# Second parts of split weights on GpSimd alone, tangents of the silu in PSUM, in a two-block transformer kernel

## The chip, the cores and the metric

The kernel runs on one core of a Trainium2 chip. The metric is the device time of one execution, in microseconds (us). Three runs of the kernel before took 2133.84, 2142.33 and 2143.69 us; their median is 2142.33 us.

## What is computed

One call runs two transformer blocks on 256 tokens of width 1024. The first block is a mixer made of a gated delta rule (GDN, 8 heads) and a state space layer (SSD, 16 heads), then a mixture of 32 experts. The second is a sparse attention with a gated linear attention, then 32 smaller experts. Everything is float32. The change lies in the first mixer, of which this much matters:

```python
proj = h @ w_in                                   # 256 x 1024 by 1024 x 6688
qkv = jax.nn.silu(causal_dwconv(gdn_qkv, gdn_conv_w))   # 3072 channels, 4 taps
q, k = l2norm(q) * (GDN_DK ** -0.5), l2norm(k)
o = gated_delta_rule_chunked(q, k, v, beta, g)    # 4 chunks of 64 tokens, a state passes on
o = rmsnorm(o, gdn_norm_g) * jax.nn.silu(gdn_z)
xbc = jax.nn.silu(causal_dwconv(ssd_xbc, ssd_conv_w) + ssd_conv_b)   # 1536 channels
y = ssd_chunked(xs, dt, a, bm, cm) + ssd_d * xs
return jnp.concatenate([o, rmsnorm(y * jax.nn.silu(ssd_z))], -1) @ w_out
```

The silu is computed as y(1 + tanh y), with y half of the convolution's result (the factor is put into the taps).

## The kernel before

**Split weights.** A float32 product is made of three matmuls in a faster type (`fp32r`): each operand is split into a first part (`wh`, `hT0`) and a rest (`wl`, `hT1`), and `mm3` adds first by first, first by rest and rest by first. `hT` is the transposed input, split once. The weights arrive in chunks of 1 MB, 128 x 2048 in SBUF (`w`). `splitter` cuts a chunk into `NSPL` = 4 parts of 512 columns: for each, ScalarE (ACT) writes `wh`, a rounded copy (L295), and then VectorE (DVE) or GpSimd (POOL) writes `wl` = `w` - `wh` (L292). `k.spd` names the parts that DVE does; it comes from the table `SPD`, one entry for each stage of the program. The first three entries hold up to the recurrence of the delta rule, and there parts 1 and 2 go to DVE and parts 0 and 3 to POOL. `wh` and `wl` have `NWH` = 2 buffers each, and a chunk is split one ahead of its use: the first piece of chunk i+2 waits until TensorE (PE) is through with chunk i.

**Stages up to the recurrence.** 23 chunks are split there. Six hold the 12 channel groups of the SSD (`xbc`), eight the keys and queries (16 groups of 128 channels), four the gate of the SSD, four the values (8 groups), and one is split ahead for the stage behind. For a chunk with two groups PE makes 48 matmuls into a PSUM tile `ps_pj` (3 buffers, `PJ`); then `conv_silu` runs once for each group.

**`conv_silu`** (L649). ACT scales the projection by the last tap (`cv_y`, L295), three DVE instructions add the other taps (L658: one input in PSUM, one in SBUF), ACT takes the tangent (`cv_t`, L295, two SBUF buffers), and DVE makes the product (L661: both inputs, `cv_t` and `cv_y`, in SBUF). PE then transposes the result (L730 for `xT`, L821 for `qk`, L1019 for `vT`), and the banks of these transposes, as of almost all small matmuls, come from a ring of five PSUM banks (`bank`, tag `g`). With `ps_pj` that is all eight banks.

**Beside it.** `ada_batch` accumulates 16 chunks of another weight on DVE (L478, 128 x 2048, both inputs in SBUF). `ssd` multiplies masks (`m`, L781 and L292) and on POOL scales `xs` and `xw`. `gdn_prep` inverts triangular blocks by doubling, a chain PE (32 x 32 matmuls, `Yc`, `Xc`, `Qc`) - DVE - PE. `weave` and `turns` interleave these generators with the projections in the text of the program; when it is built, a scheduling layer lists each engine's instructions in its own order, from the same dependences. Each engine then works through its list in order: an instruction that waits holds all behind it.

**After it.** The recurrence (`gdn_steps`), the output projection and the router follow, then the experts, whose weights stream from HBM; the second block has the same two halves.

Of the kernel before, what the change touches and what calls it, by code (L numbers as in the profile page):

```python
# [12 lines left out]
F32 = mybir.dt.float32  # L13
# [8 lines left out]
P = 128  # L22
T = 256
# [219 lines left out]
def turns(*gens):  # L243

    gens = list(gens)
    while gens:
        for g in list(gens):
            if next(g, gens) is gens:
                gens.remove(g)
        yield  # L250


def chain(*gens):
    for g in gens:
        yield from g


def weave(main, *sides):

    due = [0.0] * len(sides)  # L260
    for _ in main:
        for i, (g, rate) in enumerate(sides):
            due[i] += rate
            while due[i] >= 1:
                due[i] -= 1
                next(g, None)


def kernel_body(ctx, tc, ins, consts, out):
# [96 lines left out]
    def splitter(pool):  # L366
        def f(w):
            hi = pool.tile([P, W_CHUNK], F32R, tag="wh", bufs=NWH, name="wh")[:, :w.shape[1]]
            lo = pool.tile([P, W_CHUNK], F32R, tag="wl", bufs=NWH, name="wl")[:, :w.shape[1]]
            n = w.shape[1] // NSPL  # L370
            for i in range(NSPL):
                c = slice(i * n, (i + 1) * n)
                split_into(w[:, c], hi[:, c], lo[:, c], eng=None if i in k.spd else nc.gpsimd)
            return hi, lo
        return f

    ws.splitter = splitter(pA)
    k.spd = SPD[0]

# [173 lines left out]
    gcp = pc.tile([P, KD], F32, name="gcp")  # L553
    k.__dict__.update(locals())
    mixer1(k)
    pA.end(0)
    ps_cm.__exit__(None, None, None)
# [26 lines left out]
def mixer1(k):  # L584
    nc, tc, ws, pA = k.nc, k.tc, k.ws, k.pA
    mm, mm3, tt, act, bank, C, ident = k.mm, k.mm3, k.tt, k.act, k.bank, k.C, k.ident
# [59 lines left out]
        nc.gpsimd.tensor_copy(ac2[:, :, c:c + 16], acum)  # L646


    def conv_silu(pj, wc, ct, nct, dst, bias=None):  # L649

        y = pA.tile([P, T], F32, tag="cv_y", bufs=2, name="cv_y")
        w = lambda j: wc[:, j * nct + ct:j * nct + ct + 1]
        if bias is None:
            act(y, pj, AF.Copy, scale=w(3))
        else:
            act(y, pj, AF.Identity, scale=w(3), bias=bias)
        for s in (1, 2, 3):
            V.scalar_tensor_tensor(y[:, s:], pj[:, :T - s], w(3 - s), y[:, s:], op0=ALU.mult, op1=ALU.add)  # L658
        th = pA.tile([P, T], F32, tag="cv_t", bufs=2, name="cv_t")
        act(th, y, AF.Tanh)  # L660
        V.scalar_tensor_tensor(dst, th, 1.0, y, op0=ALU.add, op1=ALU.mult)  # L661

    def proj_ch(n, emit, emit2=None):

        for i in range(n):
            w = ws.get(split=True)
            pj = bank("pj", PJ)
            for ct in range(2):
                for kk in range(KD):
                    sl = slice(kk * 256 + ct * P, kk * 256 + ct * P + P)  # L670
                    mm3(pj[:, ct * T:(ct + 1) * T], (w[0][:, sl], w[1][:, sl]), (hT[0][:, kk], hT[1][:, kk]), start=(kk == 0), stop=(kk == KD - 1))
                if ct == 0:
                    yield
            if emit:
                for ct in range(2):
                    emit(2 * i + ct, pj[:, ct * T:(ct + 1) * T])
            else:
                emit2(i, pj)
            yield
# [44 lines left out]
    def emit(c, pj):  # L724
        if c < 8:
            xT = pA.tile([P, T], F32, tag="vT", bufs=2, name="xT")
            conv_silu(pj, cws, c, 12, xT, bias=hb[:, c:c + 1])
            pt = bank()
            for t in range(2):
                nc.tensor.transpose(pt[:, t * P:(t + 1) * P], xT[:, t * P:(t + 1) * P], ident)  # L730
                act(xs[t][:, c * P:(c + 1) * P], pt[:, t * P:(t + 1) * P], AF.Copy)
        else:
            conv_silu(pj, cws, c, 12, bc[:, c - 8], bias=hb[:, c:c + 1])
# [81 lines left out]
    def emit_kq(a):  # L815
        def f(h, pj):
            dst = qkv(h)[:, a].rearrange("p n s -> p (n s)")
            conv_silu(pj, cwg, h + (0 if a else 8), 24, dst)
            pt = bank()
            for t in range(2):  # L820
                nc.tensor.transpose(pt[:, t * P:(t + 1) * P], dst[:, t * P:(t + 1) * P], ident)  # L821
                jk = pA.tile([P, P], F32, tag="jk", bufs=1, name="jk")
                act(jk, pt[:, t * P:(t + 1) * P], AF.Square, accum_out=ssq[:, t, a * 8 + h:a * 8 + h + 1])
                if a == 0:
                    act(kd[t][:, h * P:(h + 1) * P], pt[:, t * P:(t + 1) * P], AF.Copy)
        return f
    k.spd = SPD[1]
    weave(turns(chain(proj_ch(4, emit_kq(0)), proj_ch(4, emit_kq(1))), ssd()), (ada1, RA[1]))
    run_all(ada1)
    ys = xs  # L830
    k.spd = SPD[2]

# [276 lines left out]

    k.spd = SPD[3]  # L1110
    fill = chain(proj_ch(4, None, emit_z), ssd_out)
# [6 lines left out]

    k.spd = SPD[4]

# [726 lines left out]
def mixer2(k, pool):  # L1847
# [9 lines left out]
    ws.splitter = k.splitter(pool)  # L1857
    k.spd = SPD[5]

# [690 lines left out]
NA4 = 17  # L2550
PJ = 3
NSPL = 4
SPD = ((1, 2),) * 3 + ((1, 2, 3), (1, 3), (), (1, 2), (1, 2))
RA = (0.34, 0.4, 0.25, 0.3)
FILL1 = 0.8
FILL2 = 0.6
# [55 lines left out]
```

## Time and profile before

| what | value |
|---|---|
| median of the runs | 2142.33 us |
| profiled execution, its own time | 2139.73 us |
| span of its profile | 2138.0 us |
| PE, DVE, ACT, POOL busy | 1906.9, 695.8, 438.1, 255.2 us |
| busiest split groups, whole program | POOL `wl` 180.8 us, DVE `wl` 112.4 us, ACT `wh` 139.7 us |
| HBM read | 703.69 MB, 330 GB/s over the span |

The profile is that of one execution. Busy time is what an engine's instructions took; in its share of the whole span DVE seems to have room, but most of DVE's work lies in the first 430 us and in the second mixer, while the experts between and behind them are made by PE and the weight stream. A stage is therefore read from its own stretch of the trace: who is busy there, and whom PE waits for.

### The profile page before, as it was taken

What the parts mean: (1) busy time and instruction counts of PE and PEld (TensorE: products, weight loads), DVE (VectorE), ACT (ScalarE), POOL (GpSimd) and SP (SyncE); (2) the same over time, 40 slices, a digit from 0 to 9 for tenths busy, and PEclk for the clock granted to TensorE, in tenths of its full rate; (3) what the DMA queues carried; (4) which work ended last, traced back from release to release, by engine and by line L of the source; (5) the groups of instructions that cost most, each with busy time, mean ns of one, the idle gap of its engine ahead of it and who ended that gap; (6) DMA issues with size and microseconds to landing.
All of it is one profiled execution on the core that took longest, in us unless ns stands there. A gap on an engine that the chain in (4) does not pass through costs nothing. (4 is left out here: it accounts for less than half of the span.)

```text
span 2138.0 us, 26656 instructions
## 1 busy us (share of the span) xinstructions
PE 1906.9 (89%) x10864; PEld 983.4 (46%) x10865; DVE 695.8 (33%) x1434; ACT 438.1 (20%) x1031; POOL 255.2 (12%) x202
## 2 busy tenths in 40 slices
PE   6889899699999999999999999979898788777777
PEld 3777788443343433434343433368787322212111
DVE  4988847511111211111111111375756200000001
ACT  3554524221010100001010100233543210101001
POOL 2523312200000000000000000144443000000000
PEclk8999979899999999999999999989999899999989
DMA  8654415689999999999999999936248699999997
GB/s 310 210 190 132 153 65 175 279 353 421 421 420 421 413 421 420 386 421 421 417 421 382 421 422 421 367 99 197 80 126 352 259 421 421 420 421 420 420 421 281
DMA packets 162552, 706.59 MB, mean 330 GB/s; under 512 B 20775, under 2 KB 67412, under 8 KB 87668
## 3 DMA queue, kind: packets, MB, share of 16 engines
q1 hardware_dynamic: 162420, 704.78, 83.0%
q8 instruction: 89, 1.46, 0.3%
q14 instruction: 43, 0.35, 0.0%
HBM read 703.69 MB, written 1.05 MB: 330 GB/s over the span
## 5 line engine op out<-in xcount | busy, mean ns | idle before, releaser
L282 PE MATMUL ps_gu<-w,xe 128*64 128x512 f32 (+1 forms) x3072 | 702.5, 629 | 67.8 <-DMA w<-in_w_up_dram 39.4
L282 PEld LDWEIGHTS ps_gu<-w,xe 128*64 128x64 f32 (+1 forms) x3072 | 227.6, 132 | 511.9 <-issue 373.3
L282 PE MATMUL ps_y<-w,aT 128*64 128x512 f32 (+1 forms) x1536 | 375.1, 602 | 14.8 <-DMA w<-in_w_down_dram 14.0
L292 POOL TENSOR_TENSOR wl<-w,wh 128x512 fp32r<-128x512 f32 x126 | 180.8, 1443 | 362.6 <-ACT wh L295 345.3
L282 PEld LDWEIGHTS ps_y<-w,aT 128*64 128x64 f32 (+1 forms) x1536 | 115.5, 128 | 234.1 <-issue 183.4
L1624 DVE TENSOR_SCALAR g<-ps_gu 128x512 f32<-128x512 f32 x32 | 22.0, 687 | 464.2 <-PE ps_gu L282 463.4
L295 ACT ACTIVATE wh<-w 128x512 fp32r<-128x512 f32 x244 | 139.7, 622 | 87.0 <-PE ps_pj L282 52.4
L282 PE MATMUL ps_pj<-hT,wh 128*128 128x256 f32 x704 | 143.3, 299 | 7.6 <-DVE cv_y L658 3.5
L292 DVE TENSOR_TENSOR wl<-w,wh 128x512 fp32r<-128x512 f32 x118 | 112.4, 972 | 46.0 <-ACT wh L295 42.4
L282 PEld LDWEIGHTS ps_pj<-hT,wh 128*128 128x128 f32 x704 | 116.6, 201 | 13.3 <-issue 5.5
L292 DVE TENSOR_TENSOR x<-x,ps_g 128x512 f32<-128x512 f32 x96 | 66.0, 687 | 168.1 <-PE ps_g L282 168.1
L282 PE MATMUL ps_pj<-hT,wl 128*128 128x256 f32 x352 | 105.3, 299 | 5.2 <-DVE wl L292 2.8
L295 ACT ACTIVATE g<-g 128x512 f32<-128x512 f32 x32 | 20.1, 629 | 417.9 <-DVE g L1624 417.2
L282 PE MATMUL ps_g<-ys,sgT 128*128 128x512 f32 x192 | 93.6, 616 | 1.6 <-DVE ys L292 0.8
L292 DVE TENSOR_TENSOR a<-g,ps_gu 128x512 f32<-128x512 f32 x8 | 5.5, 687 | 259.2 <-PE ps_gu L282 259.2
L282 PE MATMUL ps_g<-sel,xo 128*128 128x256 f32 x320 | 77.9, 392 | 2.0 <-ACT xe L295 1.7
L295 ACT ACTIVATE xe<-ps_g,mcol,a 128x256 f32<-128x256 f32 (+1 forms) x72 | 38.1, 539 | 190.8 <-PE ps_gu L282 150.0
L282 PEld LDWEIGHTS ps_pj<-hT,wl 128*128 128x128 f32 x352 | 71.0, 202 | 7.0 <-DVE wl L292 2.9
L282 PE MATMUL ps_pj<-uT,wh 128*128 128x256 f32 x384 | 74.0, 293 | 0.0
L292 DVE TENSOR_TENSOR ys<-ps_y,gb 128x512 f32<-128x512 f32 x32 | 22.1, 692 | 158.7 <-PE ps_y L282 158.7
L282 PEld LDWEIGHTS ps_g<-sel,xo 128*128 128x128 f32 x320 | 56.0, 189 | 31.8 <-ACT xe L295 13.3
L282 PEld LDWEIGHTS ps_pj<-uT,wh 128*128 128x128 f32 x384 | 61.5, 197 | 2.8 <-issue 1.2
(537 smaller groups left out, 1964.6 us busy)
## 6 DMA issues: line engine op xcount, KB each, us to landing
w<-in_moe_w_gu_dram SPq DMA_DIRECT2D x256, 1024.0 KB
w<-in_moe_w_down_dram SPq DMA_DIRECT2D x120, 1024.0 KB
w<-in_w_gate_dram SPq DMA_DIRECT2D x64, 1024.0 KB
w<-in_w_up_dram SPq DMA_DIRECT2D x64, 1024.0 KB
w<-in_w_down_dram SPq DMA_DIRECT2D x64, 1024.0 KB
w<-in_w_in_dram SPq DMA_DIRECT2D x45, 1024.0 KB
w<-in_ada_w_dram SPq DMA_DIRECT2D x24, 1024.0 KB
w<-in_w_out_dram SPq DMA_DIRECT2D x12, 1024.0 KB
```

Of the source, the lines that this page charges most:

```text
L282: return nc.tensor.matmul(o, l, r, start=start, stop=stop)
L292: (eng or nc.vector).tensor_tensor(o, a, b, op=op)
L295: nc.scalar.activation(o, i, f, **kw)
L1624: V.tensor_scalar(g, gu[j], 7.0, None, op0=ALU.min)
```

## The change

The tangent of `conv_silu` goes into a PSUM bank instead of an SBUF tile: a bank of the ring of five is taken for each pair of groups, the even group uses its first 256 columns, the odd one its second. And the first three entries of `SPD` become empty: up to the recurrence POOL writes `wl` of all four parts.

```diff
+    th2 = []
+
     def conv_silu(pj, wc, ct, nct, dst, bias=None):
...
-        th = pA.tile([P, T], F32, tag="cv_t", bufs=2, name="cv_t")
+        if ct % 2 == 0:
+            th2[:] = [bank()]
+        th = th2[0][:, ct % 2 * T:(ct % 2 + 1) * T]
         act(th, y, AF.Tanh)
         V.scalar_tensor_tensor(dst, th, 1.0, y, op0=ALU.add, op1=ALU.mult)
...
-SPD = ((1, 2),) * 3 + ((1, 2, 3), (1, 3), (), (1, 2), (1, 2))
+SPD = ((),) * 3 + ((1, 2, 3), (1, 3), (), (1, 2), (1, 2))
```

In the built program line numbers behind L645 move by two to four (L658 is L660, L661 is L665, L821 is L825). The order of each engine's list changes up to the recurrence and is the same behind it. Three places:

**POOL at the start**, from the first chunk on: `wl` are the weights' second parts, `hT` those of the input, which PE needs for its first chunk. Before:

```order
L292 TENSOR_TENSOR wl<-w,wh 128x512 x3
L292 TENSOR_TENSOR hT_235<-h_154,hT_234 128x256 x2
L292 TENSOR_TENSOR wl<-w,wh 128x512
L292 TENSOR_TENSOR hT_235<-h_155,hT_234 128x256 x2
L292 TENSOR_TENSOR wl<-w,wh 128x512 x3
```

Now:

```order
L292 TENSOR_TENSOR wl<-w,wh 128x512 x7
L292 TENSOR_TENSOR hT_235<-h_154,hT_234 128x256 x2
L292 TENSOR_TENSOR wl<-w,wh 128x512
L292 TENSOR_TENSOR hT_235<-h_155,hT_234 128x256 x2
L292 TENSOR_TENSOR wl<-w,wh 128x512 x8
```

Seven splits instead of three stand ahead of the first two pieces of `hT`.

**DVE at the first keys** (`qk` is the product of the silu, `bt` and `cbt` are copies for the SSD, `w<-w,cact` is the accumulation of `ada_batch`). Before:

```order
L658 SCALAR_TENSOR_TENSOR cv_y<-ps_pj,col_w,cv_y 128x254
L292 TENSOR_TENSOR wl<-w,wh 128x512
L661 SCALAR_TENSOR_TENSOR qk_868<-cv_t,cv_y 128x256
L658 SCALAR_TENSOR_TENSOR cv_y<-ps_pj,col_w,cv_y 128x253
L292 TENSOR_TENSOR wl<-w,wh 128x512
L751 COPY bt<-ps_g 128x128
L478 SCALAR_TENSOR_TENSOR w<-w,cact 128x2048
L751 COPY bt<-ps_g 128x128
L658 SCALAR_TENSOR_TENSOR cv_y<-ps_pj,col_w,cv_y 128x255
L292 TENSOR_TENSOR wl<-w,wh 128x512
L658 SCALAR_TENSOR_TENSOR cv_y<-ps_pj,col_w,cv_y 128x254
L292 TENSOR_TENSOR wl<-w,wh 128x512
```

Now:

```order
L665 SCALAR_TENSOR_TENSOR qk_862<-ps_g,cv_y 128x256
L755 COPY bt<-ps_g 128x128
L660 SCALAR_TENSOR_TENSOR cv_y<-ps_pj,col_w,cv_y 128x255
L660 SCALAR_TENSOR_TENSOR cv_y<-ps_pj,col_w,cv_y 128x254
L755 COPY bt<-ps_g 128x128
L660 SCALAR_TENSOR_TENSOR cv_y<-ps_pj,col_w,cv_y 128x253
L478 SCALAR_TENSOR_TENSOR w<-w,cact 128x2048
L765 COPY cbt<-ps_g 128x512
```

The splits are gone from DVE's list, and the product reads PSUM (`ps_g`).

**ACT at the last SSD groups** (`wh` are first parts of the next chunks). Before:

```order
L295 ACTIVATE wh<-w 128x512 x4
L295 ACTIVATE cv_t<-cv_y 128x256 x2
L295 ACTIVATE wh<-w 128x512 x2
L295 ACTIVATE cv_y<-ps_pj,hb,col_w 128x256
L295 ACTIVATE cv_y<-ps_pj,col_w 128x256
```

Now:

```order
L295 ACTIVATE wh<-w 128x512 x2
L295 ACTIVATE ps_g<-cv_y 128x256 x2
L295 ACTIVATE wh<-w 128x512 x3
L295 ACTIVATE cv_y<-ps_pj,hb,col_w 128x256
L295 ACTIVATE cv_y<-ps_pj,col_w 128x256
```

Two tangents stand side by side, and they now go into the PSUM ring.

## Rows read from the trace of the kernel before

**Rows 1.** The page's first line: span and instructions.
```profile
span 2138.0 us, 26656 instructions
```

**Rows 2.** Busy time by stretch: stretch, length; each engine's busy us (instructions); clock, DMA, GB/s.
```profile
36.00:60.00 24.00, 22.98 (x155) 19.49 (x154) 19.16 (x42) 11.09 (x24) 7.46 (x7) 0.93 0.77 256
60.00:100.00 40.00, 34.45 (x284) 33.05 (x283) 36.63 (x59) 24.23 (x62) 23.33 (x16) 1.00 0.63 212
100.00:140.00 40.00, 29.90 (x193) 26.04 (x192) 37.20 (x56) 20.65 (x63) 15.54 (x11) 0.87 0.64 211
140.00:195.00 55.00, 50.89 (x313) 40.76 (x312) 46.41 (x92) 34.83 (x105) 17.50 (x13) 1.00 0.35 115
195.00:270.00 75.00, 63.62 (x1397) 56.76 (x1399) 63.19 (x117) 33.81 (x83) 23.74 (x15) 0.93 0.49 156
...
430.00:1380.00 950.00, 934.23 (x3711) 369.60 (x3707) 160.48 (x294) 78.95 (x145) 5.68 (x7) 0.99 1.00 412
```
Engines in the row's order: PE, PE's weight loads, DVE, ACT, POOL.

**Rows 3.** Whom PE waited for from 36 to 270 us: us in total, times, longest.
```profile
PE ps_g L821 <- DVE qk L661: 6.4, 4, 4.6
PE ps_g L282 <- DVE Yc L292: 5.8, 2, 3.1
PE ps_pj L282 <- DVE cv_y L658: 3.5, 3, 2.3
...
PE ps_pj L282 <- DVE wl L292: 2.8, 1, 2.8
PE ps_g L1019 <- DVE vT L661: 2.5, 2, 1.4
PE ps_pj L282 <- POOL wl L292: 2.4, 1, 2.4
```

**Rows 4.** DVE's groups from 36 to 270 us: busy us, mean ns | idle before.
```profile
L658 DVE SCALAR_TENSOR_TENSOR cv_y<-ps_pj,col_w,cv_y 128x253 f32<-128x253 f32 (+2 forms) x108 | 48.6, 473 | 3.3 <-ACT cv_y L295 1.4 <-PE ps_g L1019 1.3
L292 DVE TENSOR_TENSOR wl<-w,wh 128x512 fp32r<-128x512 f32 x47 | 44.7, 958 | 2.1 <-ACT wh L295 1.5 <-issue 0.6
L478 DVE SCALAR_TENSOR_TENSOR w<-w,cact 128x2048 f32<-128x2048 f32 x11 | 25.8, 2343 | 2.0 <-DMA w<-in_ada_w_dram 2.0
...
L661 DVE SCALAR_TENSOR_TENSOR qk<-cv_t,cv_y 128x256 f32<-128x256 f32 x16 | 8.7, 551 | 0.1
```

**Rows 5.** POOL's splits from 36 to 270 us, same columns.
```profile
L292 POOL TENSOR_TENSOR wl<-w,wh 128x512 fp32r<-128x512 f32 x44 | 66.3, 1511 | 125.3 <-ACT wh L295 109.7 <-issue 6.1 <-PE ps_g L749 5.5
```

**Rows 6.** Durations in the whole trace, ns least/median/most: tangents, products, POOL's splits.
```profile
L295 ACT ACTIVATE cv_t<-cv_y x36: 399/417/441, 52.2 to 266.9; 128x256 f32<-128x256 f32 x36
L661 DVE SCALAR_TENSOR_TENSOR qk<-cv_t,cv_y x16: 411/418/1493, 104.2 to 184.5; 128x256 f32<-128x256 f32 x16
L292 POOL TENSOR_TENSOR wl<-w,wh x126: 1258/1309/3377, 28.3 to 1636.1; 128x512 fp32r<-128x512 f32 x126
```

**Rows 7.** Timeline at 133 us: start, length, instruction [PE's idle time before it].
```profile
132.73 1.32 POOL L292 TENSOR_TENSOR wl<-w,wh 128x512 fp32r<-128x512 f32 x1 [0.95 <-ACT wh L295]
132.85 1.48 DVE L661 SCALAR_TENSOR_TENSOR qk<-cv_t,cv_y 128x256 f32<-128x256 f32 x1
134.48 0.45 PE L821 MATMUL ps_g<-c,qk 128*128 128x128 f32 x1 [4.64 <-DVE qk L661]
```

**Rows 8.** Timeline at 65 us: an accumulation on DVE, two splits on POOL.
```profile
65.00 2.34 DVE L478 SCALAR_TENSOR_TENSOR w<-w,cact 128x2048 f32<-128x2048 f32 x1
65.09 5.07 POOL L292 TENSOR_TENSOR wl<-w,wh 128x512 fp32r<-128x512 f32 x2 [2.60 <-ACT wh L295]
```

**Rows 9.** Timeline of POOL and PE at the start.
```profile
34.36 1.27 POOL L292 TENSOR_TENSOR wl<-w,wh 128x512 fp32r<-128x512 f32 x1 [3.08 <-ACT wh L295]
36.01 1.61 POOL L292 TENSOR_TENSOR hT<-h,hT 128x256 fp32r<-128x256 f32 x2 [0.39 <-ACT hT L295]
...
42.04 0.39 PE L282 MATMUL ps_pj<-hT,wh 128*128 128x256 f32 x1 [0.56 <-POOL hT L292]
```

**Rows 10.** ACT's groups that read PSUM, from 36 to 270 us, least/median/most ns.
```profile
L295 ACT ACTIVATE cv_y<-ps_pj,col_w x24: 452/468/482, 93.1 to 262.0; 128x256 f32<-128x256 f32 x24
```

## The prediction

> **What bounds the kernel now.** I read the busy time by stretch first, then whom PE waits for, then the groups of the engine it waits for, then single pieces of the timeline. The span of the profiled execution is 2138.0 us [rows 1]; its own time is 2139.73 us, 0.12% under the median of the three runs, 2142.33 us. From 430 to 1380 us the DMA engines are busy at 1.00 of the time and move 412 GB/s, while POOL has 7 instructions [rows 2]: that stretch goes at the pace of the weight stream, and the change has nothing in it. The last row also says what time saved earlier is worth. The stream's buffers are few and it starts when the first mixer ends, so an earlier start shifts the whole rest; I count what is saved before it in full.
>
> The change works from 36 to 270 us. There DVE is busy 19.16 + 36.63 + 37.20 + 46.41 + 63.19 = 202.6 of 234 us, or 87%, and 93% from 100 to 140 us. PE is busy 201.8 us, so it stands idle for 32.2 us; ACT has 124.6 us and POOL 87.6 us [rows 2]. PE also runs partly at the lower of its two clock levels, 1.2 GHz: granted shares of 0.93, 0.87 and 0.93 over 24, 40 and 75 us make 3.4 + 10.4 + 10.5 = 24 us at that level [rows 2]. Of PE's idle time 6.4 + 5.8 + 3.5 + 2.8 + 2.5 = 21.0 us ended with DVE and 2.4 us with a split on POOL [rows 3]. So this part is bound by PE with a late DVE behind it: up to 23.4 us of waits, and some clock, can be had at most. No gain by more than about 35 us is in it.
>
> **Why DVE is late.** Two reasons, and the change aims at both. Its list is long: in this stretch 47 splits take 44.7 us, at 958 ns each, and 11 accumulations take 25.8 us [rows 4]. And it is held by POOL. The product of the silu takes 418 ns at the median but 1493 at most [rows 6], with a mean of 551 [rows 4]. One of the long ones began at 132.85 us, 0.12 us behind a split on POOL that ran until 134.05; it took 1.48 us, and PE had idled for 4.64 us when it got the result [rows 7]. Both inputs of that product were in SBUF, as were those of the split.
>
> **The change part by part.**
>
> *DVE loses 46 splits.* Two lie ahead of 36 us, and three of the 47 in the stretch belong to the stage behind; so 44 x 0.958 = 42.2 us go from the stretch [rows 4].
>
> *The 36 products read the tangent from PSUM.* The nearest row is L658, the same operation with one input in PSUM: 473 ns at 253 to 255 columns [rows 4]. If the queries' and keys' mean holds for all, 36 x (551 - 473) = 2.8 us are saved; if only the medians counted, 36 x (473 - 418) = 2.0 us would be lost. I take 2.8 saved. DVE is left with 202.6 - 42.2 - 2.8 = 157.6 of 234 us, 67%.
>
> *ACT writes 36 tangents into PSUM.* No row shows ACT writing there. Bounds: the least tangent of now, 399 ns [rows 6], and the slowest of ACT's reads from PSUM, 482 ns [rows 10], against a median of 417: between 0.6 us saved and 2.3 us lost. I take none; ACT's 124.6 of 234 us [rows 2] hide either. Without that cover the 2.3 us would count.
>
> *POOL gains 44 splits in the stretch.* At the median of 1309 ns [rows 6] that is 57.6 us, at the mean of 1511 [rows 5] 66.5 us. POOL comes to 145 to 154 of 234 us, at most 66%. A chunk then takes 4 x 1.31 to 4 x 1.51 = 5.2 to 6.0 us in one queue. Fourteen chunks are used from 36 to 195 us, one in 11.4 us, so POOL follows on the average. What can wait behind its list are the next chunk's last parts. Two buffers give a chunk the time of the one before it, so I expect a few waits of PE for POOL, together 3 us, in place of the 2.8 + 2.4 us that splits cost now.
>
> *The start.* POOL now makes two more splits ahead of the first pieces of `hT`. They began at 36.01 us, after a split at 34.36 [rows 9]; two more, at 1.27 us, move them by 2.5 us. PE waited 0.56 us for the last of these pieces at 42.04 us [rows 9]; the one split between the pairs of `hT` has slack, so I charge 1 us, bounds 0 and 2.5.
>
> *The ring of five banks* serves 18 more tiles. No row shows a wait for a bank by name; I charge nothing in the sum, and the second rival has the other end.
>
> **The sum.** Of the waits [rows 3] I take back 5 of the 6.4 us for `qk`, 2 of 3.5 for `cv_y`, 1.5 of 2.5 for `vT`, 2.2 of the 5.2 for splits, and 1.5 of the 5.8 for `Yc`. The last is little because that operation keeps both inputs in SBUF and meets more splits on POOL. That is 12.2 us. Of the clock: each us at 1.2 GHz is half a us of work at 2.4, so 24 us cost up to 12; the share of 0.87 lies in the stretch with the 4.64 us stall, and I take back 3 of the 12. Less 1 us for the start: 14 us. 2139.7 - 14 = 2125.7 by the profiled execution, 2128 by the median; I say **2127 us**. It is a sum of judged shares, so its own range is wide: from a gain of 6 to one of 25 us, 2117 to 2136.
>
> **The rivals.** A change of over 0.5% (10.7 us, about what can be told from none) begins at 2131.6 us, or at 2153.0.
>
> *All of it.* DVE gives up all its waits and the clock comes back: 23.4 + 12 - 1 = 34 us, 2108 us. For it: the 93% from 100 to 140 us [rows 2], a queue that turns every small delay into one of PE's. Against it: other waits lie just behind, and a queue at 67% still delays.
>
> *The silu's chain keeps its length: no change.* Products and tangents of a pair now share one bank. In the trace each tangent has an SBUF tile of its own and needs only its `cv_y`. If the second of a pair has to wait for the product of the first, 18 times 473 ns [rows 4] = 8.5 us are added to ACT's list, and with them to the split that stands behind (two tangents stand side by side in the new order). Together with `Yc` unchanged, 14 - 8.5 - 1.5 = 4 us are left: 2138 us. The Trainium skill (PSUM — Partial Sum Buffer, PSUM bank collisions raise a hardware error) says that ScalarE and VectorE must not be in one bank and the same partitions at once, whatever columns they touch. By that rule the wait must be there for every pair, and the time is this rival's as far as ACT is on the path; no row of the trace before shows it, since no tangent lies in PSUM there.
>
> *POOL sets the pace: slower.* Not only POOL holds DVE. The accumulation that began at 65.00 us and took 2.34 us held the first of two splits, which took 5.07 us together instead of 2 x 1.31 [rows 8]. Now POOL meets every such instruction with twice the splits. If each of the 11 accumulations held one split for its whole 2.34 us, POOL would have 154 + 26 = 180 of 234 us: still under. The point from which it decides: POOL's other work from 36 to 195 us is some 12 us, 0.9 us a chunk, so at a mean of (11.4 - 0.9) / 4 = 2.6 us for a split POOL needs all the time there is. At 3.0 us it needs 12.9 us a chunk, and 14 x 1.5 = 21 us are added: 2163 us. For it: the longest of 3377 ns [rows 6]. Against it: the mean of 1511 [rows 5], with 125 us idle before its splits. The Trainium skill (SBUF — State Buffer, Who interferes with whom) says that a VectorE instruction with two SBUF inputs and a GpSimd instruction that reads SBUF exclude each other, and that an instruction with at most one SBUF input does not contend. By that rule the tangents in PSUM free the products in full, while accumulations, masks and `Yc` still stand against twice the splits; the traces agree as far as they go, with 1.48 us and 5.07 us.
>
> **How the numbers follow.** My forecast has 0.53, of which 0.08 lies within 0.5%; all of it 0.10; no change 0.25; POOL's pace 0.12, of which 0.03 lies within 0.5%. Faster: 0.45 + 0.10 = 0.55. Within 0.5%: 0.08 + 0.25 + 0.03 = 0.36. Slower: 0.09. The range reaches down to the second case, 2106, and up past the third with the bounds of its unknown costs (2.3 us for the tangents, 2.0 for the products, 1.5 more at the start on 2138, and the runs' own 1.4 above their median): 2146. It leaves out POOL's pace and some of the lower end, under 2 in 10.
>
> **What would show it.** In the profile after: no `wl` on DVE before 260 us; products near 473 ns with none over 0.6; DVE at about 160 us for 14 us less than the 234; POOL's splits at a mean under 1.7 us; PE's waits for `qk` under 2 us; the same rows from the recurrence on, 14 us earlier. I am wrong if products still take over 1 us beside a split, if PE's waits move to `wl` on POOL with over 8 us, or if the saved time does not reach the expert stage's start.

## The result and the profile after

The changed kernel took 2158.41 us (median of 6 runs, 2153.48 to 2164.30); the kernel before took 2137.43 us in the 6 runs beside it. The ratio is 1.0090, with a 95% interval of 1.0067 to 1.0113: **slower by some 20 us**, outside the range, where a gain of 14 was forecast. The profiled execution took 2156.49 us.

First the busy time by stretch, to be held against [rows 2]; the columns are the same.

```profile
36.00:60.00 24.00, 20.68 (x131) 17.62 (x132) 14.02 (x27) 7.85 (x18) 12.24 (x11) 0.86 0.71 228
60.00:100.00 40.00, 31.09 (x227) 29.65 (x226) 26.12 (x44) 21.76 (x55) 24.59 (x20) 0.91 0.58 197
100.00:140.00 40.00, 31.75 (x203) 28.65 (x203) 23.77 (x41) 16.50 (x45) 27.89 (x19) 0.83 0.55 186
140.00:195.00 55.00, 50.15 (x314) 41.32 (x314) 38.46 (x88) 33.75 (x116) 25.89 (x21) 0.94 0.40 132
195.00:270.00 75.00, 64.57 (x1128) 56.48 (x1127) 55.16 (x102) 36.75 (x85) 49.16 (x31) 0.91 0.40 130
```

DVE did become free: 14.02 + 26.12 + 23.77 + 38.46 + 55.16 = 157.5 us instead of 202.6. Part of this difference is only that the work has slid out of the window. For the same work, from 36 us to the end of the last value's product (267.81 us before, 282.66 now), DVE is busy 166.7 us instead of 202.6: 36 us less, not 45. PE gained nothing from it: it is busy 198.2 us of the 234 instead of 201.8, and the granted clock is lower in every row, least from 195 to 270 us (0.91 for 0.93), most from 60 to 100 (0.91 for 1.00). By these shares PE ran at 1.2 GHz for 2 x (3.4 + 3.6 + 6.8 + 3.3 + 6.8) = 48 us; before it was 24. Together that is 3.6 us more idle time and 24 / 2 = 12 us of work not done, 15.6 us. The product of the last value starts at 282.23 us against 267.38 before, 14.9 us later; the recurrence's first matmul that reads the keys and queries starts at 317.2 us against 299.0, and the first copy of the experts' input (`xe`) at 448.6 against 428.3.

Whom PE waited for from 36 to 270 us (us in total, times, longest), to be held against [rows 3]:

```profile
PE ps_pj L282 <- DVE cv_y L660: 7.5, 6, 3.5
PE ps_g L282 <- issue: 6.3, 2, 3.4
PE ps_g L282 <- DVE Yc L292: 4.5, 2, 2.5
PE ps_g L825 <- DVE qk L665: 3.5, 2, 2.9
PE ps_g L734 <- DVE xT L665: 3.4, 1, 3.4
PE ps_pj L282 <- POOL wl L292: 3.1, 2, 2.1
PE ps_pj L282 <- DVE hT L292: 2.5, 2, 2.3
```

The waits for `qk` and for DVE's splits fell; waits for `cv_y`, `xT`, `hT` and one named "issue" took their place. The wait for POOL's splits is 3.1 us, as forecast, so the slower rival (POOL sets the pace) is not what happened either. Next the groups of DVE and POOL in the same stretch:

```profile
L478 DVE SCALAR_TENSOR_TENSOR w<-w,cact 128x2048 f32<-128x2048 f32 x11 | 29.1, 2648 | 14.9 <-DMA w<-in_ada_w_dram 14.9
L665 DVE SCALAR_TENSOR_TENSOR qk<-ps_g,cv_y 128x256 f32<-128x256 f32 x16 | 6.7, 420 | 4.5 <-ACT ps_g L295 4.3
L292 POOL TENSOR_TENSOR wl<-w,wh 128x512 fp32r<-128x512 f32 x84 | 118.4, 1438 | 88.7 <-ACT wh L295 84.2 <-issue 4.3
```

And the products of the keys and queries in the whole trace (ns least/median/most):

```profile
L665 DVE SCALAR_TENSOR_TENSOR qk<-ps_g,cv_y x16: 408/424/425, 111.7 to 197.4; 128x256 f32<-128x256 f32 x16
```

No product takes over 0.43 us. The accumulations (L478) now wait 14.9 us for their data, where they waited 2.0 [rows 4].

The wait "issue" is the clearest picture of what is new. It is the softplus, a chain of small DVE operations on 128 x 64; POOL first, then DVE, then PE, which needs its result `ga`:

```profile
60.66 4.97 POOL L292 TENSOR_TENSOR wl<-w,wh 128x512 fp32r<-128x512 f32 x4 [7.00 <-ACT wh L295]
...
61.08 0.97 DVE L292 TENSOR_TENSOR sp_z<-sp_z,sp_u 128x64 f32<-128x64 f32 x1
62.08 1.20 DVE L292 TENSOR_TENSOR sp_z<-sp_z,sp_e 128x64 f32<-128x64 f32 x1
63.31 1.19 DVE L2551 SCALAR_TENSOR_TENSOR spl<-sp,sp_z 128x64 f32<-128x64 f32 x1
64.53 1.17 DVE L621 SCALAR_TENSOR_TENSOR ga<-spl,ea 128x48 f32<-128x48 f32 x1
...
65.80 0.25 PE L282 MATMUL ps_g<-ga,ca 128*128 128x16 f32 x1 [3.39 <-issue]
```

Four operations of 0.21 to 0.23 us (their times before, when POOL stood idle beside them) take about as long as a split on POOL each: each ends some 0.1 us behind one of POOL's four splits, and POOL takes the next turn. That is 4.53 us instead of 0.89. PE then ran at the lower level from 67.1 to 70.5 us, a granted clock of 0.57 over 67 to 71; before it had 1.00 there. The start shows the same: beside three splits on POOL, the scaling of `h` and the pieces of `hT` on DVE are held, and PE waits 2.34 us for the first of these pieces:

```profile
33.37 3.38 DVE L537 TENSOR_SCALAR h<-h,a,mcol 128x256 f32<-128x256 f32 x4
36.67 2.36 DVE L292 TENSOR_TENSOR hT<-h,hT 128x256 fp32r<-128x256 f32 x2
...
34.05 3.82 POOL L292 TENSOR_TENSOR wl<-w,wh 128x512 fp32r<-128x512 f32 x3 [0.81 <-ACT wh L295]
```

And this is how an accumulation that waits for its weights holds the product behind it, and PE:

```profile
91.16 2.35 DVE L478 SCALAR_TENSOR_TENSOR w<-w,cact 128x2048 f32<-128x2048 f32 x1 [4.12 <-DMA w<-in_ada_w_dram]
93.42 0.42 DVE L665 SCALAR_TENSOR_TENSOR xT<-ps_g,cv_y 128x256 f32<-128x256 f32 x1
...
93.90 0.33 PE L734 MATMUL ps_g<-c,xT 128*128 128x128 f32 x1 [3.38 <-DVE xT L665]
```

The likely reason is that a chunk's buffer is given back only when its last split is done, and that POOL now makes four in a row. The waits of the DMA queue fit it: from 30 to 310 us 22 of them, 174.7 us in all, ended with a split on POOL, where before 25 of them, 186.5 us, ended with one on DVE.

### The profile page after: what moved, and what is told of

It is laid out like the page before. It is cut to its first block, busy times and chain, and to the rows that moved or that the text cites. A ratio compares the mean times of both kernels' runs of the same rounds, so it can differ in the third digit from the quotient of the medians.

```text
span 2154.7 us, 26616 instructions
## 1 busy us (share of the span) xinstructions
PE 1913.7 (89%) x10864; PEld 992.0 (46%) x10865; DVE 658.7 (31%) x1388; ACT 437.1 (20%) x1031; POOL 315.4 (15%) x248
## 5 line engine op out<-in xcount | busy, mean ns | idle before, releaser
L282 PE MATMUL ps_y<-w,aT 128*64 128x512 f32 (+1 forms) x1536 | 376.7, 602 | 15.6 <-DMA w<-in_w_down_dram 14.8
L292 POOL TENSOR_TENSOR wl<-w,wh 128x512 fp32r<-128x512 f32 x172 | 240.0, 1415 | 326.8 <-ACT wh L295 320.7
L282 PE MATMUL ps_pj<-hT,wh 128*128 128x256 f32 x704 | 152.4, 312 | 14.0 <-DVE cv_y L660 7.5
L282 PEld LDWEIGHTS ps_pj<-hT,wh 128*128 128x128 f32 x704 | 123.9, 213 | 23.3 <-DVE cv_y L660 7.1
L292 DVE TENSOR_TENSOR wl<-w,wh 128x512 fp32r<-128x512 f32 x72 | 67.7, 966 | 34.3 <-ACT wh L295 34.0
```

The costliest lines, as they stand in the source:

```text
L282: return nc.tensor.matmul(o, l, r, start=start, stop=stop)
L292: (eng or nc.vector).tensor_tensor(o, a, b, op=op)
```

## The experiments

Two theories came out of these rows. **Held operations** (A, later A2): each split on POOL holds DVE's operations with two SBUF inputs, some of which PE waits for. **Late data** (A1): buffers come free late, so accumulations wait and hold what is queued behind them. Against both stood the tangents (B), the changed order of the lists alone (C), and the length of POOL's queue (A4). Ratios are to runs of the kernel before on the same chip, with 95% intervals.

**Which half.** The tangents alone, and the splits alone:

```diff
-SPD = ((),) * 3 + ((1, 2, 3), ...
+SPD = ((1, 2),) * 3 + ((1, 2, 3), ...
```

> Only the tangents go into PSUM; the splits are shared by VectorE and GpSimd as before. Theory A, the splits: with all four parts of a chunk in GpSimd's one queue, VectorE's instructions with two SBUF inputs on the path (first pieces of the input, softplus chain) are held, the chunk's buffer comes free later, and the next weights of the accumulation arrive later while VectorE waits for them with the convolutions queued behind. Then this kernel is not slower than before: 2128 to 2140 us, products at 0.42 us, no VectorE wait for the accumulation's data over 5 us in all. Theory B, the tangents: the bank shared by two groups and 18 more tiles in the ring of five hold ACT and PE. Then this kernel carries the loss: 2150 to 2165 us. Theory C, the list order: the scheduling layer's new order is unlucky by itself; then this kernel may land anywhere, and the two parts' effects do not add up to the +21 us.

```diff
 # the kernel before
-SPD = ((1, 2),) * 3 + ((1, 2, 3), ...
+SPD = ((),) * 3 + ((1, 2, 3), ...
```

> Only the splits go to GpSimd; the tangents stay in SBUF. Theory A: the loss is here, and larger than with the tangents in PSUM, since the products are held by twice the splits again: 2158 to 2172 us, products at a mean over 0.6 us. Theory B: 2130 to 2140 us. Theory C: anything, not adding up with the other half.

The tangents alone: 2135.56 us, 0.9994 (0.9972 to 1.0017). The splits alone: 2150.67 us, 1.0063 (1.0032 to 1.0094), less than expected: theory A had them slower than the change, at 2158 us or more. So the splits carry the loss, the tangents neither lose nor gain. Theory B falls. That the products are held by POOL is true but cheap: with the splits on POOL and the tangents in SBUF they take 0.85 us on the mean, as the second row shows, and the kernel is no slower than with the tangents in PSUM.

```profile
L478 DVE SCALAR_TENSOR_TENSOR w<-w,cact 128x2048 f32<-128x2048 f32 x11 | 30.8, 2798 | 2.9 <-DMA w<-in_ada_w_dram 2.9
L661 DVE SCALAR_TENSOR_TENSOR qk<-cv_t,cv_y 128x256 f32<-128x256 f32 x16 | 13.4, 845 | 8.7 <-ACT cv_t L295 8.6
```

This run also bears on both theories. Its accumulations wait only 2.9 us for data, and its four softplus operations take 0.21 to 0.23 us each, as before: in it the loss of the splits needs neither the late data nor the held softplus.

**How many parts.** Tangents in PSUM; DVE makes part 2 alone, or parts 1, 2 and 3:

```diff
-SPD = ((),) * 3 + ((1, 2, 3), ...
+SPD = ((2,),) * 3 + ((1, 2, 3), ...
```

> The change, but part 2 of every chunk up to the recurrence stays on VectorE, the other three go to GpSimd. Theory A: three splits in GpSimd's queue are 3.9 us instead of 5.2, the chunk's buffer comes free 1.3 us earlier, and the loss is about halved: 2143 to 2152 us. Theory B: as the change, 2155 to 2162 us. Theory C: no step between, the time may lie outside the two kernels' 2137 to 2158.

```diff
-SPD = ((),) * 3 + ((1, 2, 3), ...
+SPD = ((1, 2, 3),) * 3 + ((1, 2, 3), ...
```

> Tangents in PSUM, and parts 1, 2 and 3 of each chunk up to the recurrence on VectorE, part 0 alone on GpSimd: the opposite direction. If GpSimd's splits are what costs (A2, and shown by the useless ones), and VectorE's load is not, this is as fast as before or faster: 2122 to 2137 us. If VectorE's 87% is a bound of its own, 23 more splits of 0.7 to 0.96 us make it slower: 2142 to 2155 us.

With one part on DVE: 2148.25 us, 1.0040 (1.0021 to 1.0058). With three: 2138.13 us, 0.9994 (0.9967 to 1.0021). In the order of POOL's parts, one to four, the ratios are 0.9994, 0.9994, 1.0040 and 1.0090. DVE carries 23 more splits in the first of these without loss: its load was no bound of its own.

**Where.** Tangents in PSUM, POOL's four parts in one stage only; and the change with the first three chunks as before:

```diff
+SPD = ((), (1, 2), (1, 2)) + ((1, 2, 3), ...   # e_s0
+SPD = ((1, 2), (), (1, 2)) + ((1, 2, 3), ...   # e_s1
+SPD = ((1, 2), (1, 2), ()) + ((1, 2, 3), ...   # e_s2
```

> Tangents in PSUM everywhere; GpSimd makes all four parts only in the first stage (the start and the SSD's channel groups), the two stages behind as before. With the third stage alone nothing was lost (ratio 1.0004). If the loss comes from what GpSimd holds at the start and in the softplus chain (theory A2), the larger part of it is here: 2144 to 2152 us. If it comes from late data (theory A1), whose two long waits end at 91 and at 122 us, about half: 2141 to 2147. If every stage is harmless alone and only the sum is not: 2134 to 2140.

> Tangents in PSUM everywhere; GpSimd makes all four parts only in the second stage (queries, keys and the SSD's chunks). A2: little on PE's path has two SBUF inputs there, 2135 to 2141 us. A1: the other half of the late data, 2141 to 2148 us.

> Tangents in PSUM everywhere, GpSimd makes all four parts only in the third stage (the SSD's gate, the values and the inversion, the last nine chunks); the two stages ahead as before. From the milestones of the change's profile this stage carries some 7.5 of the 20 us: 2139 to 2146 us by A2 (the inversion's two-SBUF products are held). By A1 the stage has no long wait for the accumulation's data in the change's profile (the long ones end at 91 and 122 us), so 2133 to 2139 us.

```diff
-                split_into(w[:, c], hi[:, c], lo[:, c], eng=None if i in k.spd else nc.gpsimd)
+                split_into(w[:, c], hi[:, c], lo[:, c], eng=None if i in SPC(k.nsp, k.spd) else nc.gpsimd)
+            k.nsp += 1
...
+def SPC(n, d):
+    return (1, 2) if n < 3 else d
```

> The change, but the first three chunks' parts 1 and 2 are made by VectorE as before, so that GpSimd has few splits ahead of the first pieces of the input. Theory A: the start's share comes back, that is PE's first wait of 2.3 us at 38 us, some of the 0.9 us at 44 us and 3.4 us at the lower clock (1.7 us of work): 4 to 5 us, so 2152 to 2156 us, the rest of the loss stays. Theory B: nothing or under 2 us comes back, 2156 to 2160. Theory C: a change of more than 6 us either way, since the whole list is ordered anew.

First stage 2145.52 us, 1.0033 (1.0010 to 1.0055); second 2148.96 us, 1.0054 (1.0034 to 1.0074); third 2137.55 us, 1.0004 (0.9980 to 1.0028). Measured from the tangents alone (0.9994) these are 0.39 + 0.60 + 0.10 = 1.1%, about the 0.96% of the whole: within their intervals the parts add up, which leaves little to C. The chunks at the start gave back 2.7 us (2155.70 us, 1.0078, 1.0049 to 1.0107), less than expected and within the intervals of none. The second stage was not where A2 had looked, and the third was spared; so far late data was the better theory.

**What on POOL costs.** In the next kernel DVE keeps its splits, and POOL's added work is useless:

```diff
-SPD = ((),) * 3 + ((1, 2, 3), ...
+SPD = ((1, 2),) * 3 + ((1, 2, 3), ...
...
+            jn = pool.tile([P, 512], F32, tag="jn", name="jn")
...
+            for i in (1, 2):
+                tt(jn, x[:, 0, 0:512], hi[:, i * n:(i + 1) * n].bitcast(F32), ALU.subtract, eng=nc.gpsimd)
             return hi, lo
```

> Tangents in PSUM and splits shared as before (2135.6 us in that run), and beside them GpSimd makes two useless subtractions of 128x512 for each chunk up to the recurrence (x minus part 1 and part 2 of wh, into a tile that nobody reads): GpSimd's load is that of the change, VectorE's that of before, and the weight buffers do not wait for the useless ones. Theory A1, late data: the loss comes because a chunk's buffer is given back after four splits in one queue, so that the accumulation's weights come late and VectorE, which waits for them, holds the convolutions. Then little is lost here: 2134 to 2143 us. Theory A2, the held operations: GpSimd's subtractions hold VectorE's instructions with two SBUF inputs on PE's path (input pieces, softplus, the inversion). Then most of the loss appears here: 2148 to 2162 us.

2158.10 us, 1.0085 (1.0054 to 1.0117): as large a loss as the change's, with all of DVE's splits still in place. The accumulations waited for no data up to 270 us (first row), so late data isn't needed for it; DVE's splits went from 958 ns [rows 4] to 1264. Held splits are a cost that the change doesn't have, so that the two losses are of one size is in part chance.

```profile
L482 DVE SCALAR_TENSOR_TENSOR w<-w,cact 128x2048 f32<-128x2048 f32 x10 | 27.4, 2744 | 0.0
L292 DVE TENSOR_TENSOR wl<-w,wh 128x512 fp32r<-128x512 f32 x42 | 52.8, 1264 | 2.2 <-ACT wh L295 2.0
...
L292 POOL TENSOR_TENSOR jn<-x,wh 128x512 f32<-128x512 f32 x42 | 73.2, 1743 | 2.6 <-ACT wh L295 1.2
```

Then memsets in place of the subtractions, which fill POOL's queue as well and read nothing:

```diff
+            with tc.issue_after(k.pl.ins):        # behind POOL's last split of the chunk
+                for _ in range(6):
+                    nc.gpsimd.memset(jn, 0.0)     # jn: 128x512
```

> As the run with the useless subtractions (2158.1 us), but GpSimd fills its time with six memsets of 128x512 per chunk in their place, which read no SBUF (a 128x1024 memset takes 0.95 us in the trace, so some 2.9 us per chunk against 3.5). The queue of GpSimd is as long, its own splits and the input's pieces stand behind as much. Theory A2, held operations: the memsets hold nothing of VectorE, the softplus operations are back at 0.22 us beside them, and most of the loss is gone: 2134 to 2144 us. Rival A4, the queue: what costs is that the splits stand behind other work on GpSimd; then the loss stays, 2150 to 2160 us. If the rows show VectorE's operations held beside a memset too, the run tells nothing of the two.

2142.99 us, 1.0016 (0.9996 to 1.0036). Most of the loss is gone, with POOL as busy: 132 memsets took 70.3 us, the subtractions 73.2. The two timelines show part of the difference. With memsets (POOL, then DVE):

```profile
61.00 1.57 POOL L378 TENSOR_TENSOR wl<-w,wh 128x512 fp32r<-128x512 f32 x1 [0.26 <-ACT wh L295]
62.51 3.43 POOL L382 MEMSET jn<- 128x512 f32 x6
...
61.35 1.30 DVE L292 TENSOR_TENSOR sp_z<-sp_z,sp_e 128x64 f32<-128x64 f32 x1
62.57 0.68 DVE L292 TENSOR_TENSOR wl<-w,wh 128x512 fp32r<-128x512 f32 x1
63.42 0.21 DVE L630 SCALAR_TENSOR_TENSOR ga<-spl,ea 128x48 f32<-128x48 f32 x1
...
63.62 2.35 DVE L487 SCALAR_TENSOR_TENSOR w<-w,cact 128x2048 f32<-128x2048 f32 x1
```

With the subtractions, DVE's two splits in the same place:

```profile
62.95 1.79 DVE L292 TENSOR_TENSOR wl<-w,wh 128x512 fp32r<-128x512 f32 x1
...
65.87 1.76 DVE L292 TENSOR_TENSOR wl<-w,wh 128x512 fp32r<-128x512 f32 x1
```

Beside a split, an operation of the softplus takes 1.30 us; beside the memsets 0.21, a split of DVE 0.68, and the accumulation its undisturbed 2.35. It is not the softplus in which the two runs differ: `ga` takes 0.21 us with the subtractions too. The Trainium skill (SBUF — State Buffer, Who interferes with whom) says that a VectorE instruction with two SBUF inputs contends with a GpSimd instruction that reads SBUF, not with one that only writes it; these rows agree on both counts.

**The accumulations.** Both kernels without the 14 later accumulations of `ada_batch`, and the change with accumulations that need no transfer:

```diff
-                nc.vector.scalar_tensor_tensor(acc, w, cact[:, kk:kk + 1], acc, ...)
...
+                with tc.issue_after(k.lp.ins):    # behind the last product; a_accx only
+                    nc.vector.scalar_tensor_tensor(acc, x.rearrange("p a b -> p (a b)"), cact[:, kk:kk + 1], acc, ...)
```

> The kernel before without the same 14 accumulations. VectorE was busy at 87% up to the recurrence and waited only 2.0 us for this data; 14 x 2.34 us = 33 us less on it: 2115 to 2135 us. It is the base for the run above; theory A1 and A2 expect the same here.

> The change without the 14 later accumulations of the modulation weights on VectorE (seven of eight chunks of either batch are loaded and not added; that part of the computation is left out). A1: the wait for late data and what it holds is gone, so this kernel is at most 8 us over the kernel before with the same left out. A2: GpSimd still holds the other operations, so it stays 12 us or more over it.

> The change, with the 14 later accumulations reading the resident input x in place of the weights that arrive (the sum is then another one; that part of the computation is changed, and with it the choice of experts, so that only the time up to the recurrence can be compared). They are as long and use SBUF as before, each queued behind the product that precedes it in the program, but wait for no transfer. In the change the last key is ready at 197.4 us and the last value at 282.2, in before at 184.5 and 267.4. A1: most of the 13 to 15 us comes back, last key by 190, last value by 273 us. A2: less than 4 us comes back: 194 or later, 278 or later.

Their times behind the router can't be held against the other kernels' (2541.81 us for before without accumulations, 2537.69 for the change). Against each other the change is 4 us faster there, not slower, and its last value is ready earlier, which fits A1 and not the letter of A2. The held softplus is all there in the change without accumulations, and nothing is lost by it:

```profile
63.44 1.19 DVE L2550 SCALAR_TENSOR_TENSOR spl<-sp,sp_z 128x64 f32<-128x64 f32 x1
```

These are the rows of the last value's product, of before without accumulations, of the change without, and of the change with accumulations of `x`:

```profile
262.34 0.42 DVE L660 SCALAR_TENSOR_TENSOR vT<-cv_t,cv_y 128x256 f32<-128x256 f32 x1 [0.54 <-ACT cv_t L295]
```

```profile
256.69 0.42 DVE L664 SCALAR_TENSOR_TENSOR vT<-ps_g,cv_y 128x256 f32<-128x256 f32 x1 [2.67 <-ACT ps_g L295]
```

```profile
291.43 0.43 DVE L666 SCALAR_TENSOR_TENSOR vT<-ps_g,cv_y 128x256 f32<-128x256 f32 x1 [1.88 <-ACT ps_g L295]
```

Without a transfer to wait for, the last key (202.81 us against 197.38 in the change) and the last value (against 282.23) came even later, and the recurrence started at 320.9 us against 317.2. So A1 failed its own run, though the order of DVE's list changed there too, and it was one execution. Read together: the loss needs the accumulations, but their wait is not all of it. They are DVE's longest instructions with two SBUF inputs, 29.1 us of the change's rows above; that it is their reads which meet POOL's is the likely reading, not shown by itself.

**The change itself, without what POOL reads.** DVE has no splits, POOL's queue is nearly as long, the buffer is given back behind POOL's last piece as in the change, but parts 1 and 2 of `wl` are zeros from memsets:

```diff
-                split_into(w[:, c], hi[:, c], lo[:, c], eng=None if i in k.spd else nc.gpsimd)
+                act(hi[:, c], w[:, c], AF.Copy)
+                if i in (1, 2):
+                    with tc.issue_after(k.pl.ins):
+                        for _ in range(2):
+                            nc.gpsimd.memset(lo[:, c].bitcast(F32), 0.0)
+                else:
+                    k.pl = nc.gpsimd.tensor_tensor(lo[:, c], w[:, c], hi[:, c].bitcast(F32), op=ALU.subtract)
```

> The change, but parts 1 and 2 of wl up to the recurrence are zeros, which GpSimd writes by four memsets of 128x512 between its splits of part 0 and part 3 (left out: half of the rest of the weights of these projections). VectorE has no splits, as in the change; GpSimd's queue has 2 x 1.31 + 4 x 0.53 = 4.7 us per chunk against 5.2, and the chunk's buffer is given back at its end, as in the change; but only two of the pieces read SBUF. A2, held operations: the forecast's gain comes through, as it was argued from VectorE's 42 us less: 2116 to 2134 us. Rivals A1 and A4, late data and the length of the queue: the loss stays, 2148 to 2160 us. Third case, VectorE's relief is worth nothing by itself: 2134 to 2142 us.

2139.96 us, 1.0010 (0.9984 to 1.0036). The loss is gone, so A4 falls for the change too. Late data (A1) can't be the whole either: the accumulations still wait 8.1 us for data, but that is half of the change's 14.9, so a share of it in the change is not excluded. And no gain appears: the third case. The profiled execution took 2147.58 us, 7.6 over this kernel's median, so its rows show one of the longer ones. The busy time by stretch (columns as above):

```profile
36.00:60.00 24.00, 21.12 (x120) 17.40 (x121) 15.38 (x28) 7.36 (x18) 11.48 (x14) 0.82 0.69 224
60.00:100.00 40.00, 35.23 (x280) 32.89 (x279) 28.87 (x54) 26.05 (x64) 28.44 (x34) 1.00 0.59 205
100.00:140.00 40.00, 29.94 (x212) 25.60 (x210) 26.56 (x49) 21.62 (x65) 26.82 (x30) 1.00 0.64 215
140.00:195.00 55.00, 53.30 (x316) 44.31 (x317) 38.74 (x85) 31.76 (x103) 22.51 (x28) 0.91 0.35 119
195.00:270.00 75.00, 61.95 (x1301) 54.97 (x1300) 50.34 (x106) 35.70 (x87) 41.37 (x43) 0.91 0.45 148
```

Whom PE waited for from 36 to 270 us:

```profile
PE ps_g L835 <- DVE qk L675: 5.4, 4, 2.9
PE ps_g L282 <- DVE Yc L292: 4.7, 1, 4.7
PE ps_pj L282 <- DVE cv_y L670: 3.6, 4, 1.8
...
PE ps_g L744 <- DVE xT L675: 2.5, 2, 2.1
```

And the accumulations in that stretch:

```profile
L488 DVE SCALAR_TENSOR_TENSOR w<-w,cact 128x2048 f32<-128x2048 f32 x11 | 26.1, 2373 | 8.2 <-DMA w<-in_ada_w_dram 8.1
```

DVE is busy 159.9 us, as free as in the change. PE is busy 201.5 of 234 us against 201.8 before, and it still waits 16.2 us for these four results of DVE; `qk`, `Yc` and `cv_y` alone make 13.7 us, where they made 15.7 [rows 3]. What DVE itself waits for has grown. The first row is of before, the others of this run:

```profile
DVE cv_y L658 <- ACT cv_y L295: 1.4, 3, 0.6
...
DVE cv_y L670 <- ACT cv_y L295: 6.9, 9, 1.6
DVE qk L675 <- ACT ps_g L295: 5.7, 6, 2.1
```

**Shorter pieces.** POOL's splits up to the recurrence in two pieces of 128 x 256, in the change, with the splits shared (timed twice), and with part 0 alone on POOL:

```diff
-                split_into(w[:, c], hi[:, c], lo[:, c], eng=None if i in k.spd else nc.gpsimd)
+                act(hi[:, c], w[:, c], AF.Copy)
+                for j in range(2):
+                    q = slice(i * n + j * n // 2, i * n + (j + 1) * n // 2)
+                    tt(lo[:, q], w[:, q], hi[:, q].bitcast(F32), ALU.subtract, eng=nc.gpsimd)
```

> The change, with each of GpSimd's splits up to the recurrence in two pieces of 128x256 (0.73 us each beside 1.27 for the whole). A2: what VectorE waits for, when it is held, is the end of one GpSimd instruction; with pieces of 0.73 us the softplus operations take 0.7 instead of 1.2 us, and 4 to 10 us come back: 2148 to 2155 us. Rival A4 or A1: a chunk's splits take 5.8 instead of 5.1 us in the queue, so the loss is the same or grows: 2158 to 2166 us.

> Tangents in PSUM, parts 1 and 2 on VectorE as before, GpSimd's parts 0 and 3 in pieces of 128x256. A candidate: if shorter holds are worth anything with the splits shared, 2125 to 2134 us; otherwise as with the tangents alone, 2134 to 2140 us.

> The same kernel as the run with the tangents in PSUM and GpSimd's parts 0 and 3 in pieces, timed again since its interval just took in 1 (0.9963 to 1.0006): 2128 to 2137 us if it is 0.15% under before, 2137 to 2141 if that was chance.

> Tangents in PSUM, parts 1, 2 and 3 on VectorE, GpSimd's part 0 in two pieces of 128x256. If fewer and shorter holds are worth something, as fast as or faster than the run with parts 0 and 3 in pieces (2133.4 us): 2126 to 2135; if VectorE's load decides, 2138 to 2150.

In the change 2154.51 us, 1.0080 (1.0051 to 1.0109): the softplus operations took 0.65 us beside pieces instead of 1.2, but of the 4 to 10 us expected 3.9 came back by the medians and some 2 by the ratios (1.0080 for 1.0090), within the intervals of none. With the splits shared 2133.43 us, 0.9985 (0.9963 to 1.0006), and again 2132.03 us, 0.9997 (0.9971 to 1.0022); with part 0 alone 2135.13 us, 0.9986 (0.9964 to 1.0008). None can be told from the kernel before, so no version here beats it.

## Why the prediction was wrong

- **The step that failed is the first of the sum**: "I take back 5 of the 6.4 us for `qk`, 2 of 3.5 for `cv_y`", and so on to 12.2 us, from 42 us less on DVE. DVE's load in the window, 157.5 us against a forecast of 157.6, agrees by luck: for the same work it fell by 36 us, not by 45. And its relief brought no gain: with DVE as free and POOL's reads away the ratio is 1.0010, and the lower end of its interval, 0.9984, leaves at most 3.4 of the 14 us; with 23 more splits on DVE it is 0.9994. PE's waits that end with DVE were taken for a queue that is too long. What stayed in their place were waits of DVE itself, for ACT's `cv_y` and tangents (the rows above), for PE's results and for data. That the waits are the length of the chain PE, ACT, DVE, ACT, DVE, PE is argued from those rows, not shown by a run of its own.
- **The term that was missing** is what four splits on POOL take from DVE. The prediction looked at one side: how accumulations hold POOL, and how splits held the products. The operations with two SBUF inputs that stay on DVE it named (accumulations, masks, `Yc`), but it gave them no price. Memsets in place of the reads give 1.0016 where reads give 1.0085, and 1.0010 where the change has 1.0090: 0.7 to 0.8%, 15 to 17 us. Which of the held operations carry this stays open: the loss is there without the held softplus (1.0063, the splits alone) and absent with it (the change without accumulations), so the accumulations are needed, and how they pass the delay on to PE no run shows.
- **The Trainium skill** had a sentence for this. Perfetto Trace Analysis, Optimizing Scalar/DVE Operations, says that GpSimd and VectorE share an SBUF read port, so that moving operations between the two might not help. The runs agree: moved splits gained nothing, and lost 0.6% by themselves, 0.9% with the tangents in PSUM.
- **The products in PSUM**: right in kind, better in size (420 ns, none over 430, against 473), and worth nothing that can be told: 0.9994. The rival built on the shared bank had its mechanism: in all 18 pairs the second tangent starts behind the product of the first, and one, at 70.64 us, kept ACT idle for 2.34 us. It cost nothing measurable. The tangents themselves take 0.36 to 0.39 us in PSUM, for a median of 0.417 in SBUF [rows 6], so nothing is lost there either.
- **POOL's splits**: a mean of 1438 ns (forecast 1.31 to 1.51 us), and 3.1 us of PE's waits (forecast 3). The pace was judged rightly and was not the point.
- **The start**: charged 1 us, at most 2.5. PE waited 2.5 us for DVE's pieces of `hT` and 0.9 for POOL's, where before it waited 0.4 and 0.6, and the matmul behind the last piece started at 44.63 us instead of 42.04. Only POOL's side had been priced. Giving DVE its splits back there was worth 2.7 us, if anything.
- **The clock**: 3 us were to come back. In the profiled executions 24 us more were spent at 1.2 GHz, 12 us of work. Executions differ in this (by the shares, 32 us in the run with zeros), so how the 20 us divide into waits and clock over all runs stays open.
- **What counts in full**: the loss did reach the end. The first copy of the experts' input is 20.3 us late, the whole execution 16.8. The last value alone is a rough guide to this: in the run with shared splits in pieces it came 3.1 us later than before (270.50 us), and that execution was 10 us shorter (2129.57).

## What to carry to other kernels

Before work is moved from one engine to its neighbour, look at what both read, and price the move by what it holds on the other engine: here operations of 0.2 us took 1.2 us each beside splits, and the reads of the moved work cost 15 to 17 us, while 36 us of load less brought no gain. The most visible held operation needn't be the one that costs: the held softplus was neither needed nor enough for the loss. A busy share of 87% on an engine that others wait for doesn't make its load the bound; test the relief alone, by filling the freed part with something that reads nothing, such as a memset. A useless copy of the moved work, with the old work left in place, shows the cost side in one run.

## What the runs showed of the hardware

A memset on POOL held none of the DVE operations with two SBUF inputs that were looked at: an accumulation took 2.35 us beside memsets, and 2.34 where it went first [rows 8]. Scalings with one SBUF tensor are another matter. Beside splits the four of `h` took 3.38 us (L537), where four took 1.38 before with POOL idle. Memsets held them too: in the run with six memsets a chunk, the first two of `h` took 0.65 and 0.69 us beside memsets instead of 0.41, and the first scaling of `ada_batch` took 1.65 us instead of 1.28, while a memset beside it took 1.49 instead of 0.52:

```profile
44.02 1.65 DVE L485 TENSOR_SCALAR w<-w,cact 128x2048 f32<-128x2048 f32 x1
```

So the rule as the prediction gives it, that an instruction with at most one SBUF input does not contend, is too wide for this kernel: the page (SBUF — State Buffer, Who interferes with whom, in the Trainium skill) excepts VectorE's two-port modes, and the prediction left that out. Whether the scalings ran in such a mode no run shows.

A held operation of the softplus waited for one POOL instruction and then got its turn: 1.17 to 1.20 us beside splits of 128 x 512, 0.63 to 0.66 beside pieces of 128 x 256. That is not general: in the run with zeros one scaling of `h` took 2.73 us: it began 0.08 us behind a split on POOL and ended behind that split and three memsets.
